# One level of Strassen's algorithm in the gate and up projections of a hybrid decoder block

## The chip, the cores and the metric

The kernel runs on one core of a Trainium2 chip. The metric is the device time of one execution in microseconds (us). The engines are TensorE (PE in the profile; its weight loads are PEld), VectorE (DVE), ScalarE (ACT), GpSimd (POOL) and SyncE (SP), whose queue issues all loads and stores here. A partition is one of the 128 lanes of the on-chip memory SBUF; matmuls write to accumulators in another memory, PSUM, in banks of 512 columns.

## The reference

One decoder block on 512 tokens of 1024 features. A mixer (retention and forgetting attention, merged by sigmoid gates) is followed by a SwiGLU feed-forward part with 2816 inner features, all in float32:

```python
    x = x + merged @ w_out[l]

    h2 = rmsnorm(x, g_ffn[l])
    ff = (jax.nn.silu(h2 @ w_gate[l]) * (h2 @ w_up[l])) @ w_down[l]
    x = x + ff
```

`rmsnorm(x, g)` divides each token's row by its root mean square and multiplies by the gains g. The change touches the two products with `w_gate` and `w_up`, each 512 x 1024 by 1024 x 2816, and what feeds and reads them.

## The kernel before, in words

To reach float32 accuracy, every float32 factor of a large product is split into a high part (a cast to the format fp32r, on ScalarE) and a low part (the value less its high part, on VectorE). One product of two tiles is then three matmuls into one accumulator (`three`, L156): high by high, high by low, low by high. Each matmul has its own weight load.

From the output projection on, features lie on partitions and tokens are the 512 moving columns; the weights are stationary, 128 x 128 at a time. `feat` (L507) makes two tiles of 128 output features: it loads the weights in units of four k-tiles (128 x 1024, 512 KB, `load_w` L133), splits each (`split_raw` L139: cast on L143, subtraction on L144), and goes over the eight k-tiles of 128 features of the input, 8 x 2 x 3 = 48 matmuls of 512 columns, two accumulators of one bank each. `three` calls `mm` (L70), so all matmuls stand on L71 in the profile.

The stages that matter here:

- Output projection (L642 to L664): four calls of `feat`. At the end of each, `evac_o` adds the residual on VectorE (L654), multiplies by the feed-forward gains and casts on ScalarE (L655, the tile `xgh`), makes the low part on VectorE (L656, `xgl`), squares on ScalarE (L661) and adds the squares into `sqs` on GpSimd (L662).
- Gate and up (L668 to L698): 11 pairs of feature tiles. For each pair `feat` makes the gate, then up, 22 calls in all. `evac_g` multiplies the gate's accumulator by `r2`, the inverse root mean square per token, on VectorE (L678) and applies silu on ScalarE (L679). `evac_u` multiplies up by `r2` on VectorE (L684), and GpSimd multiplies the two into `pf` (L685), two operations of 512 columns per pair. `r2` is made during the first gate from `sqs` by a matmul with ones and Newton's steps on tiles of 128 x 512 (L692, L693).
- Down projection (L700 to L725): for each of 22 k-tiles the weights and `pf` are split (L710 to L714), and 24 matmuls go to eight accumulators.

The order of instructions within an engine is made by the language's scheduler from the data's dependences and the order in the program; each engine then works through its own list in that order and stands still where the next one waits. The buffers of a tile name (a tag) are used in turn; a new tile waits until all readers of the one in its place are done.

Of the kernel before, what the change touches and what calls it, by code (L numbers as in the profile page):

```python
# [9 lines left out]
F32 = mybir.dt.float32  # L10
# [42 lines left out]
def block_kernel(ctx: ExitStack, tc, x, xT, c_early, c_tab, c_late, w_qf, w_tok, w_a, w_y, w_o, w_gu, w_dn, out):  # L53
# [27 lines left out]
    hp = tc.alloc_tile_pool(name="hp", bufs=1, side="left")  # L81
# [4 lines left out]
    sm = ctx.enter_context(tc.tile_pool(name="sm", bufs=2, side="right"))  # L86
    orp = tc.alloc_tile_pool(name="orp", bufs=1, side="right")
# [14 lines left out]
    def rsqrt(dst, ss, inv_n, shape, nm, pool=None):  # L102
        """(ss * inv_n + eps) ** -0.5 on the Vector engine: a guess from the exponent, then Newton's steps."""
        v = (pool or sm).tile(shape, F32, name=nm + "v", tag=nm + "v", bufs=1 if pool else 2)
        yi = (pool or sm).tile(shape, I32, name=nm + "y", tag=nm + "y", bufs=1 if pool else 2)
        a = (pool or sm).tile(shape, F32, name=nm + "a", tag=nm + "a", bufs=1 if pool else 2)
        y = yi.bitcast(F32)
        ts(out=v, in0=ss, scalar1=inv_n, scalar2=EPS, op0=ALU.mult, op1=ALU.add)
        ts(out=yi, in0=v.bitcast(I32), scalar1=1, scalar2=None, op0=ALU.logical_shift_right)
        ts(out=yi, in0=yi, scalar1=-1.0, scalar2=float(0x5F3759DF), op0=ALU.mult, op1=ALU.add)  # L110
        for i in range(3):
            stt(out=a, in0=y, scalar=-0.5, in1=y, op0=ALU.mult, op1=ALU.mult)
            tt(out=a, in0=a, in1=v, op=ALU.mult)
            stt(out=dst if i == 2 else y, in0=a, scalar=1.5, in1=y, op0=ALU.add, op1=ALU.mult)

# [107 lines left out]
    def tok_group(src, evac, cuts=(512,), ahead=()):  # L223
        """A projection with tokens on partitions: columns in cuts of one bank, src the units of 1024 / cut k-tiles each."""
# [20 lines left out]
    class Fill:  # L245
# [152 lines left out]
    def head_norm(z):  # L398
        """The heads' root mean squares: collected over the token tiles, applied after the last."""
# [36 lines left out]
    def fox_prep(a, part):  # L436
        """q or k of a pair of heads, with features on partitions, in high and low parts."""
# [21 lines left out]
    def fox_scores(a, e, i):  # L459
        """A block of queries of a head, the last block first: its row of the softmax, normalised."""  # L460
# [23 lines left out]
    def fox_turn(a, e, i):  # L484
        """That row with the keys on partitions: blocks j = 0..i at columns j*384 + i*128."""
# [21 lines left out]
    def feat(src, nu, mh, ml, evac):  # L507
        """Two tiles of features: src the units of 4 k-tiles each."""
# [130 lines left out]
    orp.release()  # L639

# [1 line left out]
    xp = tc.alloc_tile_pool(name="xp", bufs=1, side="right")  # L642
    xgh = xp.tile([P, NK, S], F32R, name="xgh")
    xgl = xp.tile([P, NK, S], F32R, name="xgl")
    x1 = xp.tile([P, NK, S], F32, name="x1")
    r2 = xp.tile([P, S], F32, name="r2")
    sqs = xp.tile([P, S], F32, name="sqs")
    for i in range(4):
        nc.sync.dma_start(out=x1[:, 2 * i:2 * i + 2, :], in_=xT[:, 2 * i:2 * i + 2, :])
    for mp in range(4):  # L650
        def evac_o(m2, acc):
            m = 2 * mp + m2
            xn = x1[:, m, :]
            tt(out=xn, in0=acc, in1=xn, op=ALU.add)  # L654
            act(out=xgh[:, m, :], in_=xn, func=AF.Copy, scale=gffn(m))  # L655
            stt(out=xgl[:, m, :], in0=xn, scalar=gffn(m), in1=f32(xgh)[:, m, :], op0=ALU.mult, op1=ALU.subtract)  # L656
            if m == 0:
                act(out=sqs, in_=xn, func=AF.Square)
            else:
                sq2 = xp.tile([P, S], F32, name="sq2", tag="sq2", bufs=2)  # L660
                act(out=sq2, in_=xn, func=AF.Square)  # L661
                gp.tensor_tensor(out=sqs, in0=sqs, in1=sq2, op=ALU.add)  # L662
        run(feat(lambda u: w_o[mp, u], 2, mgh, mgl, evac_o))
    mgp.release()  # L664
    hp.release()

# [1 line left out]
    fp = tc.alloc_tile_pool(name="fp", bufs=1, side="left")  # L668
    pf = fp.tile([P, NF, S], F32, name="pf")
    raw_pools += [fp]  # L670
    part_pools += [fp, fp]
    turns[:] = [0, 0]
    for f2 in range(NF // 2):
        gts = []

        def evac_g(m2, acc):
            gt = fp.tile([P, S], F32, name="gt", tag="fa", bufs=5)
            tt(out=gt, in0=acc, in1=r2, op=ALU.mult)  # L678
            act(out=gt, in_=gt, func=AF.Silu)  # L679
            gts.append(gt)  # L680

        def evac_u(m2, acc):
            up = fp.tile([P, S], F32, name="up", tag="fb", bufs=5)
            tt(out=up, in0=acc, in1=r2, op=ALU.mult)  # L684
            gp.tensor_tensor(out=pf[:, 2 * f2 + m2, :], in0=up, in1=gts[m2], op=ALU.mult)  # L685

        if f2 == 0:
            waiting = []
            for n, _ in enumerate(feat(lambda u: w_gu[0, f2, u], 2, xgh, xgl, lambda m2, acc: waiting.append(acc))):
                if n == 9:  # L690
                    pb = bank("tp")
                    mm(pb, lhsT=ones, rhs=sqs, start=True, stop=True)  # L692
            rsqrt(r2, pb, 1.0 / D, [P, S], "n2", xp)  # L693
            for m2, acc in enumerate(waiting):
                evac_g(m2, acc)
        else:
            run(feat(lambda u: w_gu[0, f2, u], 2, xgh, xgl, evac_g))
        run(feat(lambda u: w_gu[1, f2, u], 2, xgh, xgl, evac_u))  # L698
# [9 lines left out]

    for k in range(NF):
        h, l = split_w(w_dn[k])  # L710
        ph = fp.tile([P, S], F32R, name="ph", tag="fa", bufs=5)
        pl = fp.tile([P, S], F32R, name="pl", tag="fb", bufs=5)
        nc.scalar.copy(out=ph, in_=pf[:, k, :])
        tt(out=pl, in0=pf[:, k, :], in1=f32(ph), op=ALU.subtract)  # L714
        parts.append((h, l, ph, pl))
# [3 lines left out]
    for m in range(NK):  # L719
        for k in range(NF - TAIL, NF):  # L720
            down(k, m)
        ot = fp.tile([P, S], F32, name="ot", tag="fa", bufs=5)
# [3 lines left out]
    fp.release()  # L726
    xp.release()
    ps.release()
    drp.release()
    wp.release()  # L730
# [4 lines left out]
def _constants():  # L735
# [6 lines left out]
    ex = lambda a: np.exp(a.astype(f).astype(np.float64)).astype(f)  # noqa: E731  # L742
# [23 lines left out]
def _layout(i):  # L766
# [13 lines left out]
    def fm(m):  # L780
        """[K, N] -> [N/256, K/512, 128, 4*256]"""
        k, n = m.shape
        return m.reshape(k // 512, 4, P, n // 256, 256).transpose(3, 0, 2, 1, 4).reshape(n // 256, k // 512, P, 1024)

    qf = np.zeros((4, P, 4 * 264), f)
    for u in range(4):
# [12 lines left out]
        "w_gu": np.stack([fm(a["w_gate"][0]), fm(a["w_up"][0])]),  # L799
        "w_dn": a["w_down"][0].reshape(NF, P, D),  # L800
# [19 lines left out]
```

## Time and profile before

| What | Value |
| --- | --- |
| median time of 3 runs (753.85 to 753.88) | 753.86 us |
| span of the profiled execution | 750.1 us |
| time less span: what lies around it | 3.76 us |
| output projection and what is around it, 345.0 to 376.5 | 31.5 us |
| gate and up, 376.5 to 623.7 | 247.2 us |
| down projection and the end, 623.7 to 750.0 | 126.3 us |

The profile shows one execution, its span from the first to the last instruction; the execution's own time outside the profiler is not given, so the median stands for it. A row of a group gives the source line, the engine, the operation, output<-inputs with partitions x columns, the number of instructions, then the busy time in us, the mean ns of one, and the idle time of the engine ahead of them with what ended it. A row of a tile gives the least, median and longest duration in ns. A row of a timeline gives the start, the length of the merged instructions and, in brackets, the idle time before and what ended it.

### The profile page before, as it was taken

The page shows a single profiled execution, that of the slowest core. Times are in us where ns is not written, and L with a number is a line of the kernel's source. Part 1 is how long each engine was busy: PE and PEld are TensorE (multiplying, and loading weights), DVE is VectorE, ACT ScalarE, POOL GpSimd, SP SyncE. Part 2 cuts the span into 40 slices and gives each one's busy share as a digit, 9 for nine tenths or more (in the row PEclk, how much of TensorE's full clock was granted, in tenths as well). Part 3 has the DMA queues.
Part 4 walks back from the last instruction along what each step waited for, and adds up shares of the span by engine and source line. Part 5 has one row for each costly group of instructions (what it writes and reads, how often), then busy time and mean ns, then how long its engine had stood idle before and what let it go on. Part 6 is the DMA issues. An engine that isn't in the chain of part 4 may idle for free.

```text
span 750.1 us, 8828 instructions
## 1 busy us (share of the span) xinstructions
PE 742.7 (99%) x3430; PEld 596.9 (80%) x3430; DVE 367.7 (49%) x630; ACT 259.8 (35%) x389; POOL 110.0 (15%) x112
## 2 busy tenths in 40 slices
PE   8999999999999999999999999999999999999998
PEld 5888997878777788888878888888888887888886
DVE  6424567757878644454585333334334236323212
ACT  4532442447676622223333222222122233222210
POOL 0243502212222000000311110111111011000000
PEclk9999999999999999999999999999999999999999
DMA  8532221242320132235243232232232322222203
GB/s 306 207 128 76 78 85 56 85 124 75 113 85 29 57 107 90 86 97 210 91 154 121 86 109 87 90 107 85 95 102 84 100 98 84 96 101 84 85 0 113
DMA packets 23354, 76.20 MB, mean 102 GB/s; under 512 B 2697, under 2 KB 3081, under 8 KB 23313
## 3 DMA queue, kind: packets, MB, share of 16 engines
q1 hardware_dynamic: 23312, 75.64, 30.1%
q8 instruction: 27, 0.44, 0.2%
q14 instruction: 15, 0.11, 0.1%
HBM read 73.52 MB, written 2.11 MB: 101 GB/s over the span
## 4 chain that ended last, share of the span: by engine, by line
PE 93%; DVE 3%; ACT 2%; issue 1%; DMA 1%; SPq 0%; DVEq 0%; ACTq 0%
PE acc L71 76%; PE sc L71 9%; PE tp L71 6%; PE tp L74 2%; DVE wl L144 1%; ACT pr L479 1%; DMA xf<-in_xT_dram 1%; DVE pr L477 0%; ACT wh L143 0%; ACT pT L496 0%; DVE pr L481 0%; DVE tq L456 0%; ACT tq L455 0%; DVE up L684 0%; ACT tk L446 0%
## 5 line engine op out<-in xcount | busy, mean ns | idle before, releaser
L143 ACT CAST wh<-raw 128x1024 fp32r<-128x1024 f32 (+1 forms) x118 | 123.6, 1050 | 393.3 <-PE acc L71 323.3
L144 DVE TENSOR_TENSOR wl<-raw,wh 128x1024 fp32r<-128x1024 f32 (+1 forms) x118 | 153.3, 1300 | 201.3 <-ACT wh L143 199.9
L71 PE MATMUL acc<-xgh,wh 128*128 128x512 f32 x352 | 139.5, 396 | 0.0
L71 PE MATMUL acc<-xgh,wl 128*128 128x512 f32 x352 | 139.2, 395 | 0.0
L71 PE MATMUL acc<-xgl,wh 128*128 128x512 f32 x352 | 138.8, 394 | 0.0
L71 PEld LDWEIGHTS acc<-xgh,wl 128*128 128x128 f32 x352 | 66.2, 188 | 16.1
L71 PEld LDWEIGHTS acc<-xgl,wh 128*128 128x128 f32 x352 | 66.0, 188 | 16.3 <-issue 0.2
L71 PEld LDWEIGHTS acc<-xgh,wh 128*128 128x128 f32 x352 | 66.1, 188 | 15.8 <-issue 0.2
L71 PE MATMUL acc<-wh,xh 128*128 128x512 f32 (+2 forms) x192 | 70.3, 366 | 0.0
L685 POOL TENSOR_TENSOR pf<-up,gt 128x512 f32<-128x512 f32 x22 | 38.3, 1760 | 206.0 <-DVE up L684 206.0
L71 PE MATMUL acc<-wl,xh 128*128 128x512 f32 (+2 forms) x192 | 68.4, 356 | 0.0
L71 PE MATMUL acc<-wh,xl 128*128 128x512 f32 (+2 forms) x192 | 68.3, 356 | 0.0
L71 PE MATMUL acc<-xh,wh 128*128 128x512 f32 x128 | 52.0, 406 | 0.0
L71 PE MATMUL acc<-xh,wl 128*128 128x512 f32 x128 | 50.7, 396 | 0.0
L71 PE MATMUL acc<-xl,wh 128*128 128x512 f32 x128 | 50.5, 395 | 0.0
L71 PEld LDWEIGHTS acc<-wh,xh 128*128 128x128 f32 x192 | 36.1, 188 | 5.9 <-issue 0.3
L71 PEld LDWEIGHTS acc<-wh,xl 128*128 128x128 f32 x192 | 36.1, 188 | 5.7
L71 PEld LDWEIGHTS acc<-wl,xh 128*128 128x128 f32 x192 | 36.1, 188 | 4.7
L71 PE MATMUL acc<-pl,wh 128*128 128x512 f32 x88 | 34.5, 392 | 0.0
L71 PE MATMUL acc<-ph,wl 128*128 128x512 f32 x88 | 34.5, 392 | 0.0
L71 PE MATMUL acc<-ph,wh 128*128 128x512 f32 x88 | 34.3, 393 | 0.0
L662 POOL TENSOR_TENSOR sqs<-sqs,sq 128x512 f32<-128x512 f32 x7 | 11.6, 1651 | 127.4 <-ACT sq L661 127.2
(215 smaller groups left out, 1127.2 us busy)
## 6 DMA issues: line engine op xcount, KB each, us to landing
raw<-in_w_gu_dram SPq DMA_DIRECT2D x44, 512.0 KB, 3.5
raw<-in_w_dn_dram SPq DMA_DIRECT2D x22, 512.0 KB, 3.5
raw<-in_w_tok_dram SPq DMA_DIRECT2D x16, 512.0 KB, 3.7
raw<-in_w_a_dram SPq DMA_DIRECT2D x16, 512.0 KB, 3.5
raw<-in_w_y_dram SPq DMA_DIRECT2D x8, 512.0 KB, 3.5
raw<-in_w_o_dram SPq DMA_DIRECT2D x8, 512.0 KB, 3.6
xf<-in_xT_dram SPq DMA_DIRECT2D x8, 256.0 KB, 5.8
xs<-in_x_dram SPq DMA_DIRECT2D x2, 1024.0 KB, 9.3
```

The source lines that it names most:

```text
L71: in_order(nc.tensor.matmul(o, **kw))
L74: in_order(nc.tensor.transpose(out=o, in_=src, identity=ident))
L143: nc.scalar.copy(out=h[:, :width], in_=raw[:, :width])
L144: tt(out=l[:, :width], in0=raw[:, :width], in1=f32(h)[:, :width], op=ALU.subtract)
L479: fox["last"] = act(out=pr[:, :n], in_=pr[:, :n], func=AF.Exp, scale=-1.0, bias=nm, accum_out=rs)
L662: gp.tensor_tensor(out=sqs, in0=sqs, in1=sq2, op=ALU.add)
L685: gp.tensor_tensor(out=pf[:, 2 * f2 + m2, :], in0=up, in1=gts[m2], op=ALU.mult)
```

## The change

Gate and up are made by one level of Strassen's algorithm, in the form of Winograd (seven products, with sums that share parts). The weights of one call are seen as 2 x 2 blocks (the two k-tiles of a pair by the two feature tiles), the activations likewise (the two k-tiles of a pair by two halves of 256 tokens). Eight block products become seven, each 4 k-pairs x 3 matmuls = 12 matmuls of 256 columns: 84 where there were 48 of 512.

- Activations: `evac_o` leaves x1 with its gains in `fx`; per pair of k-tiles VectorE makes the four combinations S1 to S4 (256 columns each), and the seven blocks are split in two goes of three and four slots (`split_x`: cast on ScalarE, subtraction on VectorE). This is done once, beside and behind the output projection.
- Weights: `factors` loads 1 MB (four blocks of 512 columns) for one step, that is gate or up of one pair of feature tiles. VectorE makes four combinations T1 to T4, and the three plain blocks and the four combinations are split: casts of 1536, 1024 and 1024 columns on ScalarE, subtractions of the same size on VectorE. The tiles `raw`, `ah` and `al` (plain blocks) have two buffers, `ts`, `ch0`, `cl0` (T2, T1) and `ch1`, `cl1` (T4, T3) one each. `factors` for step n + 1 stands in the program ahead of the products of step n.
- Products: `winograd` runs three single products, then T2 x S2 into the accumulator x that ScalarE has copied out once (`u`), T1 x S1 into z, T3 x S3 into x after a second copy, T4 x A22 into y, and a third copy. VectorE makes the outputs `d` from y, z and the copies in three operations (512, 256, 512 columns).
- The multiplications by `r2` leave VectorE: for the gate GpSimd multiplies `d` by `r2`, ScalarE applies silu, GpSimd multiplies by `r2` again; for up GpSimd multiplies by `d`. These are three operations of 1024 columns per pair. `r2` comes from four matmuls of one column and Newton's steps on 128 x 4.
- The first step takes the products over the first three k-pairs ahead of those over the fourth.
- Around it: `xh` and `xl` and the new pools lie elsewhere in memory; the down projection's weights come two k-tiles to a load, its parts use the buffers of `ch0`, `ah`, `ch1`, `ah` in turn.

The core of the diff:

```diff
     for mp in range(4):
+        fx = tmp.tile([P, 8, HT], F32, name="fx", tag="fx")
...
         run(feat(lambda u: w_o[mp, u], 2, mgh, mgl, evac_o))
+        split_x(mp, fx, 0, 3)
+        tt(out=fx[:, S1, :], in0=fx[:, A21, :], in1=fx[:, A22, :], op=ALU.subtract)
+        tt(out=fx[:, S2, :], in0=fx[:, S1, :], in1=fx[:, A11, :], op=ALU.subtract)
+        tt(out=fx[:, S3, :], in0=fx[:, A11, :], in1=fx[:, A21, :], op=ALU.subtract)
+        tt(out=fx[:, S4, :], in0=fx[:, S2, :], in1=fx[:, A12, :], op=ALU.add)
+        split_x(mp, fx, 3, 7)
...
+    def factors(src):
+
+        raw, ts4 = wtile("raw"), wtile("ts")
+        nc.sync.dma_start(out=raw, in_=src)
+        a = split_to(raw[:, 1:4, :], ("ah", "al"))
+        tt(out=ts4[:, 1:4:2, :], in0=raw[:, 1:4:2, :], in1=raw[:, 0:1, :].broadcast_to([P, 2, 512]), op=ALU.add)
+        tt(out=ts4[:, T2, :], in0=ts4[:, T1, :], in1=raw[:, B22, :], op=ALU.add)
+        c0 = split_to(ts4[:, 0:2, :], ("ch0", "cl0"))
+        tt(out=ts4[:, T4, :], in0=ts4[:, T2, :], in1=raw[:, B21, :], op=ALU.add)
+        c1 = split_to(ts4[:, 2:4, :], ("ch1", "cl1"))
+        return {"B11": (a, 0), "B21": (a, 1), "B22": (a, 2), "T2": (c0, 0), "T1": (c0, 1), "T4": (c1, 0), "T3": (c1, 1)}
+
+    def product(o, w, slot, new, js=range(4)):
+        (h, l), i = w
+        for j in js:
+            fs = slice(j * P, (j + 1) * P)
+            for n, (st, mv) in enumerate(((h, xfh), (h, xfl), (l, xfh))):
+                first = new and j == 0 and n == 0
+                mm(o, lhsT=st[:, i, fs], rhs=mv[j][:, slot, :], start=first, stop=j == 3 and n == 2, skip_group_check=not new)
+
+    def winograd(w, early=False):
+
+        x, y, z = bank("sc"), bank("acc"), bank("acc")
+        u = fp.tile([P, 3, HT], F32, name="u", tag="u", bufs=2)
+        d = fp.tile([P, 2, S], F32, name="d", tag="d", bufs=3)
+        lo, hi = slice(0, HT), slice(HT, S)
+        singles = ((x[:, lo], w["B11"], A11), (y[:, lo], w["B21"], A12), (z[:, hi], w["B22"], S4))
+        for js in ((range(3), range(3, 4)) if early else (range(4),)):
+            for o, f, s in singles:
+                product(o, f, s, True, js)
+        nc.scalar.copy(out=u[:, 0, :], in_=x[:, lo])
+        product(x[:, lo], w["T2"], S2, False)
+        product(z[:, lo], w["T1"], S1, True)
+        nc.scalar.copy(out=u[:, 1, :], in_=x[:, lo])
+        product(x[:, lo], w["T3"], S3, False)
+        product(y[:, hi], w["T4"], A22, True)
+        nc.scalar.copy(out=u[:, 2, :], in_=x[:, lo])
+        tt(out=d[:, 1, :].rearrange("p (s t) -> p s t", s=2), in0=z[:, lo].rearrange("p (o t) -> p o t", o=1).broadcast_to([P, 2, HT]), in1=u[:, 1:3, :], op=ALU.subtract)
+        tt(out=d[:, 1, lo], in0=z[:, hi], in1=d[:, 1, lo], op=ALU.add)
+        tt(out=d[:, 0, :].rearrange("p (s t) -> p s t", s=2), in0=y.rearrange("p (s t) -> p s t", s=2), in1=u[:, 0:3:2, :], op=ALU.add)
+        return d
...
+    for n in range(NF):
+        f2, g = n // 2, n % 2
+        if n < NF - 1:
+            ws.append(factors(w_gu[(n + 1) % 2, (n + 1) // 2]))
+        d = winograd(ws[n], n == 0)
...
+        pp = pf[:, 2 * f2:2 * f2 + 2, :]
+        if g == 0:
+            gp.tensor_tensor(out=d, in0=d, in1=r2b, op=ALU.mult)
+            act(out=pp, in_=d, func=AF.Silu)
+            gp.tensor_tensor(out=pp, in0=pp, in1=r2b, op=ALU.mult)
         else:
-            run(feat(lambda u: w_gu[0, f2, u], 2, xgh, xgl, evac_g))
-        run(feat(lambda u: w_gu[1, f2, u], 2, xgh, xgl, evac_u))
+            gp.tensor_tensor(out=pp, in0=pp, in1=d, op=ALU.mult)
```

More of the change, by code (lines that the diff above doesn't have):

```diff
@@ L80, in block_kernel @@
     wp = tc.alloc_tile_pool(name="wp", bufs=1, side="left")
-    hp = tc.alloc_tile_pool(name="hp", bufs=1, side="left")
     ftok = tc.alloc_tile_pool(name="ftok", bufs=1, side="left")
@@ L86, in block_kernel @@
     sm = ctx.enter_context(tc.tile_pool(name="sm", bufs=2, side="right"))
+    hp = tc.alloc_tile_pool(name="hp", bufs=1, side="right")
     orp = tc.alloc_tile_pool(name="orp", bufs=1, side="right")
@@ L639, in block_kernel, with split_x @@
     orp.release()
+    hp.release()
+    HT = S // 2
     xp = tc.alloc_tile_pool(name="xp", bufs=1, side="right")
-    xgh = xp.tile([P, NK, S], F32R, name="xgh")
-    xgl = xp.tile([P, NK, S], F32R, name="xgl")
     x1 = xp.tile([P, NK, S], F32, name="x1")
     r2 = xp.tile([P, S], F32, name="r2")
-    sqs = xp.tile([P, S], F32, name="sqs")
+    xfh = [xp.tile([P, 7, HT], F32R, name="xfh", tag=f"xfh{j}") for j in range(4)]
+    xfl = [xp.tile([P, 7, HT], F32R, name="xfl", tag=f"xfl{j}") for j in range(4)]
+    wq = tc.alloc_tile_pool(name="wq", bufs=1, side="right")
+    tmp = tc.alloc_tile_pool(name="tmp", bufs=1, side="left")
+    sqs = r1
+    A11, A12, A22, S1, S2, S3, S4, A21 = range(8)
     for i in range(4):
         nc.sync.dma_start(out=x1[:, 2 * i:2 * i + 2, :], in_=xT[:, 2 * i:2 * i + 2, :])
+    def split_x(j, f, lo, hi):
+        nc.scalar.copy(out=xfh[j][:, lo:hi, :], in_=f[:, lo:hi, :])
+        tt(out=xfl[j][:, lo:hi, :], in0=f[:, lo:hi, :], in1=f32(xfh[j])[:, lo:hi, :], op=ALU.subtract)
     for mp in range(4):
+        fx = tmp.tile([P, 8, HT], F32, name="fx", tag="fx")
         def evac_o(m2, acc):
@@ L654, in evac_o @@
             tt(out=xn, in0=acc, in1=xn, op=ALU.add)
-            act(out=xgh[:, m, :], in_=xn, func=AF.Copy, scale=gffn(m))
-            stt(out=xgl[:, m, :], in0=xn, scalar=gffn(m), in1=f32(xgh)[:, m, :], op0=ALU.mult, op1=ALU.subtract)
+            act(out=fx[:, 0:8:7, :] if m2 == 0 else fx[:, 1:3, :], in_=xn.rearrange("p (s t) -> p s t", s=2), func=AF.Copy, scale=gffn(m))
             if m == 0:
@@ L659, in evac_o @@
             else:
-                sq2 = xp.tile([P, S], F32, name="sq2", tag="sq2", bufs=2)
+                sq2 = tmp.tile([P, S], F32, name="sq2", tag="sq2")
                 act(out=sq2, in_=xn, func=AF.Square)
@@ L663, in block_kernel @@
         run(feat(lambda u: w_o[mp, u], 2, mgh, mgl, evac_o))
+        split_x(mp, fx, 0, 3)
[4 more added lines that the diff above has]
+        split_x(mp, fx, 3, 7)
+    B12, B11, B21, B22 = range(4)
+    T2, T1, T4, T3 = range(4)
@@ new lines, in block_kernel, with wtile, split_to @@
+    wpools = [wq]
+    WT = {"raw": (4, F32), "ts": (4, F32), "ah": (3, F32R), "al": (3, F32R),
+          "ch0": (2, F32R), "cl0": (2, F32R), "ch1": (2, F32R), "cl1": (2, F32R)}
+    seen = {}
+    def wtile(tag):
+        n, dt = WT[tag]
+        two = tag in ("raw", "ah", "al") and len(wpools) > 1
+        i = seen.get(tag, 0)
+        seen[tag] = i + 1
+        return wpools[i % 2 if two else 0].tile([P, n, 512], dt, name=tag, tag=tag)
+    def split_to(src, tags):
+        h, l = wtile(tags[0]), wtile(tags[1])
+        nc.scalar.copy(out=h, in_=src)
+        tt(out=l, in0=src, in1=f32(h), op=ALU.subtract)
+        return h, l
@@ L664, in block_kernel @@
+    ws = [factors(w_gu[0, 0])]
+    tmp.release()
     mgp.release()
-    hp.release()
+    wp.release()
     fp = tc.alloc_tile_pool(name="fp", bufs=1, side="left")
+    wpools += [fp]
     pf = fp.tile([P, NF, S], F32, name="pf")
[L670 to L695, printed above, removed]
-        else:
-            run(feat(lambda u: w_gu[0, f2, u], 2, xgh, xgl, evac_g))
-        run(feat(lambda u: w_gu[1, f2, u], 2, xgh, xgl, evac_u))
@@ new lines, in block_kernel @@
+    r2b = r2.rearrange("p (o t) -> p o t", o=1).broadcast_to([P, 2, S])
+    for n in range(NF):
[3 more added lines that the diff above has]
+        d = winograd(ws[n], n == 0)
+        if n == 0:
+            pb = bank("tp")
+            for t in range(NT):
+                mm(pb[:, t:t + 1], lhsT=sqs[:, t * P:(t + 1) * P], rhs=ones[:, 0:1], start=True, stop=True)
+            rstd2 = sm.tile([P, NT], F32, name="rstd2", tag="rstd2", bufs=1)
+            rsqrt(rstd2, pb[:, 0:NT], 1.0 / D, [P, NT], "n1")
+            broadcast_cols(rstd2, r2)
+        pp = pf[:, 2 * f2:2 * f2 + 2, :]
[3 more added lines that the diff above has]
+            gp.tensor_tensor(out=pp, in0=pp, in1=r2b, op=ALU.mult)
+        else:
+            gp.tensor_tensor(out=pp, in0=pp, in1=d, op=ALU.mult)
@@ L707, in down @@
         three(accs[m], h[:, fs], l[:, fs], ph, pl, k == 0, k == NF - 1)
+    raw = None
     for k in range(NF):
[L710 to L715, printed above, removed]
+        if k % 2 == 0:
+            raw = wtile("raw")
+            nc.sync.dma_start(out=raw, in_=w_dn[k // 2])
+        src = raw[:, 2 * (k % 2):2 * (k % 2) + 2, :]
+        tags = (("ch0", "cl0"), ("ah", "al"), ("ch1", "cl1"), ("ah", "al"))[k % 4]
+        h, l = (wtile(t)[:, 0:2, :] for t in tags)
+        nc.scalar.copy(out=h, in_=src)
+        tt(out=l, in0=src, in1=f32(h), op=ALU.subtract)
+        hl = fp.tile([P, 2, S], F32R, name="hl", tag="d", bufs=3)
+        nc.scalar.copy(out=hl[:, 0, :], in_=pf[:, k, :])
+        tt(out=hl[:, 1, :], in0=pf[:, k, :], in1=f32(hl)[:, 0, :], op=ALU.subtract)
+        h, l = (a.rearrange("p a b -> p (a b)") for a in (h, l))
+        parts.append((h, l, hl[:, 0, :], hl[:, 1, :]))
         if k < NF - TAIL:
@@ L721, in block_kernel @@
             down(k, m)
-        ot = fp.tile([P, S], F32, name="ot", tag="fa", bufs=5)
+        ot = fp.tile([P, S], F32, name="ot", tag="u", bufs=2)
         for cs in (slice(0, S),) if m < NK - 1 else (slice(0, S // 2), slice(S // 2, S)):
@@ L726, in block_kernel @@
     fp.release()
+    wq.release()
     xp.release()
@@ L729, in block_kernel @@
     drp.release()
-    wp.release()
     cst.release()
@@ L783, in fm, with wino @@
         return m.reshape(k // 512, 4, P, n // 256, 256).transpose(3, 0, 2, 1, 4).reshape(n // 256, k // 512, P, 1024)
+    def wino(m):
+        k, n = m.shape
+        v = m.reshape(k // 256, 2, P, n // 256, 2, P)
+        v = np.stack([v[:, 0, :, :, 1], v[:, 0, :, :, 0], v[:, 1, :, :, 0], v[:, 1, :, :, 1]])
+        return v.transpose(3, 2, 0, 1, 4).reshape(n // 256, P, 4, k // 2)
     qf = np.zeros((4, P, 4 * 264), f)
@@ L798, in _layout @@
         "w_o": fm(a["w_out"][0]),
-        "w_gu": np.stack([fm(a["w_gate"][0]), fm(a["w_up"][0])]),
-        "w_dn": a["w_down"][0].reshape(NF, P, D),
+        "w_gu": np.stack([wino(a["w_gate"][0]), wino(a["w_up"][0])]),
+        "w_dn": a["w_down"][0].reshape(NF // 2, 2, P, 2, D // 2).transpose(0, 2, 1, 3, 4).reshape(NF // 2, P, 4, D // 2),
     }
```

## The prediction

> **What bounds the kernel now.** I read the page first, for the share of each engine and the chain that ended last.
>
> ```profile
> span 750.1 us, 8828 instructions
> PE 742.7 (99%) x3430; PEld 596.9 (80%) x3430; DVE 367.7 (49%) x630; ACT 259.8 (35%) x389; POOL 110.0 (15%) x112
> PE 93%; DVE 3%; ACT 2%; issue 1%; DMA 1%; SPq 0%; DVEq 0%; ACTq 0%
> ```
>
> TensorE is busy for all but 7.4 us of the span, and it is 93% of the chain. But these are averages, so next comes the view of busy time by stretch. The three stretches are the output projection, gate and up, and the down projection:
>
> ```profile
> core 0: us, PE busy (x) PEld busy (x) DVE busy (x) ACT busy (x) POOL busy (x), PEclk, DMA share, GB/s
> 345.00:376.50 31.50, 31.50 (x138) 25.64 (x137) 15.85 (x17) 11.46 (x16) 8.13 (x5) 1.00 0.35 117
> 376.50:623.70 247.20, 247.20 (x1060) 198.90 (x1059) 101.51 (x105) 64.85 (x76) 38.71 (x22) 1.00 0.31 100
> 623.70:750.00 126.30, 122.31 (x529) 98.83 (x527) 43.52 (x51) 28.98 (x37) 2.98 (x2) 0.99 0.23 79
> ```
>
> Gate and up take 247.2 us, and TensorE never pauses there, at a granted clock of 1.00. They are 22 steps (11 pairs of feature tiles, gate and up each) of 48 matmuls with 512 moving columns: 1056 matmuls, 234 ns each, 11.24 us a step. VectorE works 101.5 of the 247 us and GpSimd 38.7. That room is what the change spends.
>
> **TensorE's part.** A step becomes 84 matmuls of 256 columns: seven products of four k-pairs, three partial products each. The q projection already runs such matmuls, a new weight load before each. The timeline of TensorE has 38 of them in a row; these are the first and the last:
>
> ```profile
> 82.52 0.28 PE L71 MATMUL acc<-wl,xh 128*128 128x256 f32 x1
> 86.88 0.28 PE L71 MATMUL acc<-wh,xl 128*128 128x256 f32 x1
> ```
>
> 37 intervals in 4.36 us are 117.8 ns, half of 234. Weight loads do not get in the way at this size. So 22 x 84 x 117.8 ns = 217.7 us: TensorE alone would save 29.5 us.
>
> **VectorE's part.** Every step now makes four more weight combinations and splits seven blocks in place of four. Per step and partition VectorE does, with both inputs in SBUF: the low part of three blocks (1536 columns), T1 and T3 (1024), T2 (512), the low part of T2 and T1 (1024), T4 (512), the low part of T4 and T3 (1024). Then, from PSUM, three sums: 512, 256 and 512 columns. The rows that price these:
>
> ```profile
> L144 DVE TENSOR_TENSOR wl<-raw,wh 128x1024 fp32r<-128x1024 f32 x3 | 3.7, 1225 | 4.0 <-ACT wh L143 4.0
> L714 DVE TENSOR_TENSOR pl<-pf,ph x22: 680/684/1760, 624.5 to 720.8; 128x512 fp32r<-128x512 f32 x22
> L684 DVE TENSOR_TENSOR up<-acc,r 128x512 f32<-128x512 f32 x22 | 15.2, 692 | 28.5 <-PE acc L71 28.5
> L340 DVE TENSOR_TENSOR sT<-sc,cl 128x256 f32<-128x256 f32 x8 | 3.0, 420 | 5.1 <-PE sc L71 5.0
> 345.54 1.41 DVE L656 SCALAR_TENSOR_TENSOR xgl<-x,ce,xgh 128x512 fp32r<-128x512 f32 x2
> ```
>
> From 1225 ns for 1024 columns and a median of 684 for 512 (in the view of the tile pf), 512 more cost 541, so 1536 columns are 1.77 us. The six SBUF operations are 1.77 + 3 x 1.225 + 2 x 0.684 = 6.81 us, the three sums 0.692 + 0.420 + 0.692 = 1.80: together 8.61. Back to back, two operations overlap by 0.08 us (two of 745 in 1.41); were all six to do so it would be 8.13. Some depend on the one ahead, so I take 8.4 us, 6.6 of it weights. That is under TensorE's 9.90 (84 x 117.8 ns): alone, VectorE would be hidden.
>
> **GpSimd's part decides.** Before, GpSimd multiplied two tiles of 512 columns per gate-and-up pair. Now it does three of 1024: the gate's sum by r2, its silu by r2, and the product with up. How VectorE and GpSimd get on stands in the views of the tiles xgl and pf and in the timelines:
>
> ```profile
> L656 DVE SCALAR_TENSOR_TENSOR xgl<-x,ce,xgh x8: 743/745/1789, 345.5 to 379.8; 128x512 fp32r<-128x512 f32 x8
> 356.71 2.45 DVE L656 SCALAR_TENSOR_TENSOR xgl<-x,ce,xgh 128x512 fp32r<-128x512 f32 x2
> 356.81 3.49 POOL L662 TENSOR_TENSOR sqs<-sqs,sq 128x512 f32<-128x512 f32 x2 [8.72 <-ACT sq L661]
> L685 POOL TENSOR_TENSOR pf<-up,gt x22: 1290/1520/2283, 400.3 to 625.3; 128x512 f32<-128x512 f32 x22
> 488.97 1.39 DVE L684 TENSOR_TENSOR up<-acc,r 128x512 f32<-128x512 f32 x2 [2.78 <-PE acc L71]
> 489.80 3.52 POOL L685 TENSOR_TENSOR pf<-up,gt 128x512 f32<-128x512 f32 x2 [18.86 <-DVE up L684]
> 490.56 1.62 DVE L144 TENSOR_TENSOR wl<-raw,wh 128x1024 fp32r<-128x1024 f32 x1 [0.20 <-ACT wh L143]
> L309 POOL TENSOR_TENSOR ta<-rz,cl 128x256 f32<-128x256 f32 x4 | 3.0, 738 | 28.1 <-ACT rz L273 28.0
> ```
>
> At 345 us, with GpSimd idle, two xgl took 1.41; at 356.7, beside one GpSimd operation that got in between, 2.45, so VectorE lost 1.04 us to it. At 490 the same happens to the low part of a weight (1.62 for 1.225), and GpSimd's second multiplication takes up to 2.28 where 1.29 is its least. But the two operations at 488.97 that read an accumulator in PSUM took 1.39, undisturbed. So an operation with both inputs in SBUF and one of GpSimd take turns, and only the sums from PSUM can lie beside GpSimd.
>
> By size, GpSimd takes 738 ns for 256 columns and 1290 for 512, so 2.39 us for 1024, and VectorE's loss grows from 1.04 to 2.14. Three of these per pair of steps are 6.4 us. Can they lie beside the sums? The first follows its own sum, so the next operation on VectorE is a weight's. The second follows silu: at the latest 0.14 for the hand-off, 1.77 waiting for a VectorE operation, 2.39, and silu, about 1.05, some 5.4 us after the sum. The next sums are six weight operations (6.6) and a turn (2.14) away. The third follows up's sum like the first. So I count no overlap:
>
> two steps: 2 x 8.4 + 6.4 = 23.2 us, 11.6 a step, against TensorE's 9.90 and the 11.24 of before.
>
> The Trainium skill, page "SBUF — State Buffer", section "SBUF: two separate sides", says that VectorE with two SBUF inputs and GpSimd contend for one pair of ports, an exclusive lock held for the whole instruction, the loser fully blocked. Charged with the whole 2.39 of each GpSimd operation, the sum by the page would be 8 us longer than mine over 32 of them, about 774; the 1.04 of the row is shorter than the 1.29 of the operation, and I go by the row.
>
> **ScalarE.** Its rows:
>
> ```profile
> L143 ACT CAST wh<-raw 128x1024 fp32r<-128x1024 f32 x3 | 3.1, 1049 | 9.0 <-PE acc L71 9.0
> L713 ACT CAST ph<-pf 128x512 fp32r<-128x512 f32 x22 | 13.3, 615 | 1.7 <-POOL pf L685 1.7
> L496 ACT COPY pT<-tp 128x256 f32<-128x256 f32 x8 | 2.9, 365 | 1.4 <-PE tp L74 1.2
> ```
>
> Casts of 1536, 1024 and 1024 columns are 1.48 + 2 x 1.05 us, three copies out of PSUM 3 x 0.365, silu 0.52 a step on average: 5.2 of 11.6 us. The second copy must end while TensorE does the product T1 x S1 (12 x 117.8 ns = 1.41 us), or TensorE waits; 0.37 fits unless a cast or a waiting silu stands ahead of it.
>
> **DMA.** The bytes are the same, in 22 transfers of 1 MB instead of 44 of half; at 100 GB/s in this stretch, nothing. One place is late: the second step's raw weights go into memory that the output projection's operands hold, so SyncE's queue stands there until 376.3, with the third step's load behind it.
>
> ```profile
> raw<-in_w_gu_dram SPq DMA_DIRECT2D x44, 512.0 KB, 3.5
> ```
>
> At twice 3.5 us they land by 383.3, when VectorE still has x to split (below), so this is hidden; uncovered it would cost up to 7 us once.
>
> **The start of the stage.** Before, x's last tile was split beside running matmuls. Now the last tile pair has to be summed into S1 to S4 before any product over the fourth k-pair:
>
> ```profile
> 376.23 1.39 DVE L654 TENSOR_TENSOR x<-acc,x 128x512 f32<-128x512 f32 x2 [2.78 <-PE acc L71]
> L655 ACT ACTIVATE xgh<-x,ce 128x512 fp32r<-128x512 f32 x8 | 5.7, 713 | 0.0
> L661 ACT ACTIVATE sq<-x 128x512 f32<-128x512 f32 x7 | 4.3, 615 | 0.0
> ```
>
> From 376.2: residual 1.4, the second gain copy 0.9 later (713 ns and the hand-off), a square 0.6, the cast of three slots (768 columns) 0.83, their low part 0.95, four sums of 256 columns 4 x 0.41, a cast 1.05, a low part 1.23: 8.6 us, with one square's turn on GpSimd (1.04) hidden in what can be reordered; 7 at best, 10 at worst. TensorE has 33 matmuls (3.9 us) meanwhile, so it waits some 4.5 us. Weights of the first step are prepared earlier, beside the output projection, where VectorE is half idle (15.85 of 31.5 us).
>
> **The sum.** VectorE from 376.3 on: 8.7 until x is split, then 21 weight sets x 6.6 = 138.6, 21 sums x 1.8 = 37.8, 32 turns x 2.14 = 68.5, and twelve small operations for r2, priced by this row at 12 x 0.295 = 3.5:
>
> ```profile
> L112 DVE SCALAR_TENSOR_TENSOR n4a<-n4y 128x4 f32<-128x4 f32 x12 | 3.5, 295 | 0.4
> ```
>
> Together 248.4. Then TensorE's last two products, 2.8. The end of the stage is at 376.3 + 8.7 + 248.4 + 2.8 = 636.2, against 623.7: +12.5 us. The down projection has the same matmuls; its 4.0 us of waiting (126.30 less 122.31) I leave. Stages ahead only move in memory: nothing. Span 762.6. The median of 753.86 lies 3.8 above the span of 750.1, so 766.4: **766 us**. Own range of this case: 759 (all operations overlapping, 21 x 0.27, and x split in 7) to 778 (none overlapping, 21 x 0.21, and the turns as long as the whole operation, 32 x 0.25).
>
> **The rivals.**
> *TensorE keeps the pace* (chance 0.18): if GpSimd's operations find VectorE idle or at its sums, two steps need no more than 19.8. Then 753.9 - 29.5 + 4.5 = 729. It decides from the point where 3.4 of the 6.4 us per pair are hidden. Against it: the order of dependence above, and that the sums offer only 3.6.
> *Half hidden* (0.15): silu comes late, and its second multiplication falls on the next sums: 1.8 saved per pair, 11 x 1.8 = 20 us: 745, with the scatter of the terms 740 to 755.
> *ScalarE's queue* (0.09): silu at the head of ScalarE waits for GpSimd, the second copy stands behind it, and TensorE for that; 1 to 2 us in each of 11 gates on top of my sum: 777 to 788.
> *Matmuls of 256 columns at the pace of their weight loads* (0.02): each load lasts 188 ns, 1848 x 188 = 347 us, +100: 854. The 117.8 ns speak against it.
>
> ```profile
> L71 PEld LDWEIGHTS acc<-xgh,wh 128*128 128x128 f32 x352 | 66.1, 188 | 15.8 <-issue 0.2
> ```
>
> **How the numbers follow.** The forecast has 0.56. A measurement tells 0.2% (1.5 us) from no change. Slower: the forecast without its lowest part (0.51), ScalarE's queue and the loads: 0.62. Within 0.2%: 0.03 each from forecast and half hidden: 0.06. Faster: 0.18, 0.12 and 0.02 from the forecast: 0.32. The range 733 to 780 leaves out over half of the first rival (0.10) and the upper ends (0.07 to 0.08).
>
> **What would show it.** Right: VectorE over 90% busy between 385 and 636, its SBUF operations with maxima 2 us over their minima, GpSimd's of 1024 columns near 2.4 at least; TensorE pausing in each step, ended by VectorE's low part of T4 and T3 (or T2 and T1); about 11.6 us a step; a pause of 4 to 5 us near 380. Wrong: TensorE at 99% with steps of 9.9, or pauses ended by ScalarE's copies.

## The result, and the profile after

The changed kernel takes 761.26 us (median of 4 runs, 760.69 to 761.47) against 753.86 before: slower, the ratio of the runs on record 1.0108 with a 95% interval of 1.0093 to 1.0123 (the two medians alone give 1.0098). The forecast was 766 us, slower.

The first lines of the page of the changed kernel, span and busy time of each engine:

```profile
span 759.0 us, 10565 instructions
PE 727.8 (96%) x4232; PEld 629.5 (83%) x4232; DVE 527.2 (69%) x760; ACT 320.1 (42%) x475; POOL 170.5 (22%) x123
```

TensorE has lost 14.9 us of work and the span has grown by 8.9: it waits now. VectorE has gained 159.5 us and GpSimd 60.5. Averages over the span do not say who sets the pace, so next comes the busy time by stretch (the output projection, two pieces of the stage's start, its body, the down projection):

```profile
core 0: us, PE busy (x) PEld busy (x) DVE busy (x) ACT busy (x) POOL busy (x), PEclk, DMA share, GB/s
345.00:376.50 31.50, 31.50 (x137) 25.66 (x136) 28.71 (x32) 18.44 (x24) 7.71 (x5) 1.00 0.34 123
376.50:384.00 7.50, 5.94 (x47) 5.61 (x46) 6.48 (x9) 4.26 (x6) 2.55 (x2) 1.00 0.00 0
384.00:386.00 2.00, 2.00 (x12) 2.00 (x11) 1.74 (x9) 0.84 (x2) 0.00 (x0) 0.52 0.46 70
390.00:628.00 238.00, 217.19 (x1734) 214.06 (x1733) 230.63 (x191) 105.65 (x137) 95.38 (x31) 0.97 0.27 94
634.10:759.00 124.90, 120.02 (x529) 98.71 (x527) 46.19 (x54) 30.55 (x40) 2.71 (x1) 1.00 0.27 93
```

In the body VectorE is busy for 230.6 of 238 us, 97%: it is full. Gate and up now end at 634.1, 257 us after the output projection's end where it was 247 before. From step 1 to step 21 the timeline of TensorE gives the pace; these are the first matmuls of the two steps:

```profile
392.68 0.38 PE L71 MATMUL sc<-xfh,ah 128*128 128x256 f32 x1 [1.01 <-ACT ah L701]
623.68 0.28 PE L71 MATMUL sc<-xfh,ah 128*128 128x256 f32 x1
```

20 steps in 231.0 us are 11.55 each; 11.6 was forecast.

What fills VectorE is seen in its groups between 390 and 620 us, with GpSimd's three multiplications (the columns are those of the groups before):

```profile
L710 DVE TENSOR_TENSOR ts<-raw 128x1024 f32<-128x1024 f32 x21 | 59.0, 2810 | 1.1 <-DMA raw<-in_w_gu_dram 0.6
L702 DVE TENSOR_TENSOR cl<-ts,ch 128x1024 fp32r<-128x1024 f32 x40 | 49.8, 1250 | 0.8 <-ACT ch L701 0.8
L702 DVE TENSOR_TENSOR al<-raw,ah 128x1536 fp32r<-128x1536 f32 x20 | 38.1, 1907 | 1.9 <-ACT ah L701 1.9
L713 DVE TENSOR_TENSOR ts<-ts,raw 128x512 f32<-128x512 f32 x20 | 32.4, 1619 | 0.6
L711 DVE TENSOR_TENSOR ts<-ts,raw 128x512 f32<-128x512 f32 x21 | 18.7, 889 | 0.7
L769 POOL TENSOR_TENSOR d<-d,r 128x1024 f32<-128x1024 f32 x10 | 32.3, 3234 | 80.9 <-DVE d L744 62.0 <-ACT r L220 18.9
L771 POOL TENSOR_TENSOR pf<-pf,r 128x1024 f32<-128x1024 f32 x10 | 27.8, 2783 | 12.6 <-ACT pf L770 12.6
L773 POOL TENSOR_TENSOR pf<-pf,d 128x1024 f32<-128x1024 f32 x10 | 32.5, 3254 | 50.7 <-DVE d L744 41.2 <-DVE d L743 9.5
```

Two groups of the same shape, `ts` and `cl` with 1024 columns, take 2810 and 1250 ns: the first stands where GpSimd's turn falls, the second hardly ever. The busy time of VectorE holds waiting. The three sums from PSUM keep their length throughout. None of them ran beside a multiplication in this kernel, so that they could do so undisturbed is shown by the kernel before alone (the two of 488.97 in the prediction). This is the view of the tile d, least, median and longest:

```profile
L742 DVE TENSOR_TENSOR d<-acc,u x22: 674/678/691, 391.3 to 634.4; 128x512 f32<-128x512 f32 x22
L744 DVE TENSOR_TENSOR d<-acc,u x22: 673/681/685, 395.9 to 635.9; 128x512 f32<-128x512 f32 x22
```

The view of the waits, though, names another cause of TensorE's pauses (engine and line waiting <- what ended it: us in total, times, longest):

```profile
PE sc L71 <- ACT u L738: 17.2, 8, 4.3
PE sc L71 <- DVE cl L702: 2.1, 3, 1.0
```

The second copy of the accumulator x on ScalarE ends most pauses, and VectorE few. The timelines of one step show why (step 11, from 508 us on):

```profile
511.66 3.31 POOL L769 TENSOR_TENSOR d<-d,r 128x1024 f32<-128x1024 f32 x1 [7.08 <-DVE d L744]
512.75 3.31 DVE L710 TENSOR_TENSOR ts<-raw 128x1024 f32<-128x1024 f32 x1
515.00 1.06 ACT L770 ACTIVATE pf<-d 128x1024 f32<-128x1024 f32 x1 [5.04 <-POOL d L769]
515.97 1.45 ACT L701 CAST ah<-raw 128x1536 fp32r<-128x1536 f32 x1
516.14 2.86 POOL L771 TENSOR_TENSOR pf<-pf,r 128x1024 f32<-128x1024 f32 x1 [1.17 <-ACT pf L770]
516.82 2.73 DVE L713 TENSOR_TENSOR ts<-ts,raw 128x512 f32<-128x512 f32 x1
517.33 0.36 ACT L738 COPY u<-sc 128x256 f32<-128x256 f32 x1
517.74 0.58 PE L71 MATMUL sc<-xfh,ch 128*128 128x256 f32 x1 [2.44 <-ACT u L738]
```

GpSimd's first multiplication holds VectorE's `ts` until 515; silu on ScalarE waits for it, a cast of 1.45 us follows, then the copy, and TensorE has stood 2.44 us. So two theories were to be told apart. The turns theory, the forecast's: VectorE and GpSimd take turns, and their sum is the pace, whoever ends TensorE's pauses. The chain theory, the rival of ScalarE's queue: TensorE waits because silu waits for GpSimd with the copy behind it. It costs 17 to 19 us whatever VectorE's load.

### The profile page after: what moved, and what is told of

Read it like the earlier page. It is cut to its first block, busy times and chain, and to the rows that moved or that the text cites. A ratio compares the mean times of both kernels' runs of the same rounds, so it can differ in the third digit from the quotient of the medians.

```text
span 759.0 us, 10565 instructions
## 1 busy us (share of the span) xinstructions
PE 727.8 (96%) x4232; PEld 629.5 (83%) x4232; DVE 527.2 (69%) x760; ACT 320.1 (42%) x475; POOL 170.5 (22%) x123
## 4 chain that ended last, share of the span: by engine, by line
PE 71%; DVE 14%; issue 5%; POOL 4%; ACT 4%; DMA 1%; SPq 0%; DVEq 0%; ACTq 0%; POOLq 0%
PE acc L71 48%; PE sc L71 15%; PE tp L71 6%; POOL d L769 4%; DVE cl L702 3%; PE tp L74 2%; DVE ts L710 2%; DVE al L702 2%; ACT ah L701 1%; DVE d L742 1%; DVE d L744 1%; DVE d L743 1%; DVE ts L711 1%; DMA out_dram<-ot 1%; DMA raw<-in_w_tok_dram 1%
## 5 line engine op out<-in xcount | busy, mean ns | idle before, releaser
L143 ACT CAST wh<-raw 128x1024 fp32r<-128x1024 f32 (+1 forms) x52 | 54.5, 1050 | 128.2 <-PE acc L71 100.7
L144 DVE TENSOR_TENSOR wl<-raw,wh 128x1024 fp32r<-128x1024 f32 (+1 forms) x52 | 67.8, 1305 | 46.1 <-ACT wh L143 45.9
L71 PE MATMUL sc<-xfh,ch 128*128 128x256 f32 x176 | 53.2, 302 | 17.7 <-ACT u L738 17.2
L710 DVE TENSOR_TENSOR ts<-raw 128x1024 f32<-128x1024 f32 x22 | 60.2, 2737 | 1.1 <-DMA raw<-in_w_gu_dram 0.6
L702 DVE TENSOR_TENSOR cl<-ts,ch 128x1024 fp32r<-128x1024 f32 x44 | 54.6, 1247 | 0.8 <-ACT ch L701 0.8
L71 PE MATMUL sc<-xfh,cl 128*128 128x256 f32 x176 | 52.0, 295 | 2.1 <-DVE cl L702 2.1
L71 PE MATMUL sc<-xfl,ch 128*128 128x256 f32 x176 | 51.8, 294 | 0.0
L71 PE MATMUL acc<-xfh,ch 128*128 128x256 f32 x176 | 51.2, 291 | 0.0
L71 PE MATMUL acc<-xfl,ch 128*128 128x256 f32 x176 | 50.8, 289 | 0.0
L71 PE MATMUL acc<-xfh,cl 128*128 128x256 f32 x176 | 50.7, 288 | 0.0
```

The source lines that it names most:

```text
L71: in_order(nc.tensor.matmul(o, **kw))
L143: nc.scalar.copy(out=h[:, :width], in_=raw[:, :width])
L144: tt(out=l[:, :width], in0=raw[:, :width], in1=f32(h)[:, :width], op=ALU.subtract)
L702: tt(out=l, in0=src, in1=f32(h), op=ALU.subtract)
L710: tt(out=ts4[:, 1:4:2, :], in0=raw[:, 1:4:2, :], in1=raw[:, 0:1, :].broadcast_to([P, 2, 512]), op=ALU.add)
```

## The experiments

All changes are to the changed kernel. Times are medians; ratios are to the kernel before, on the same chip (752.5 to 753.2 us there).

**Silu freed from GpSimd.** The multiplication keeps its size and place but writes aside.

```diff
-            gp.tensor_tensor(out=d, in0=d, in1=r2b, op=ALU.mult)
+            aside = pf[:, 2 * f2 + 2:2 * f2 + 4, :] if f2 < NF // 2 - 1 else d
+            gp.tensor_tensor(out=aside, in0=d, in1=r2b, op=ALU.mult)
             act(out=pp, in_=d, func=AF.Silu)
```

> Silu reads the sums directly; GpSimd's first multiplication by r2 still runs, at the same size, into a part of pf that is written again later, so silu lacks r2. Turns theory (VectorE and GpSimd take turns, and their sum of 23.1 us per two steps is the pace): nothing is taken off either engine, so 755 to 762 us; VectorE's idle 7 us in the stage is the most there is to win. Chain theory (TensorE waits because silu waits for GpSimd and the second copy stands behind silu on ScalarE): the 17 to 19 us that TensorE waited for that copy go, about 742 us.

761.44 us (761.17 to 762.63), the changed kernel's time. The chain is broken and nothing is won: TensorE now pauses ahead of T2 x S2 instead, for 15.0 us in 9 waits ended by the first copy. A pause's releaser is the last in a row of things that are all late. VectorE stays full, 207.05 of 210 us:

```profile
390.00:600.00 210.00, 192.05 (x1543) 188.61 (x1542) 207.05 (x169) 92.77 (x123) 87.19 (x27) 0.98 0.27 92
```

**Memsets for multiplications.** Here `d` stands for the gate's and up's sum.

```diff
-            gp.tensor_tensor(out=d, in0=d, in1=r2b, op=ALU.mult)
+            for _ in range(3):
+                gp.memset(d, 1.0)
             act(out=pp, in_=d, func=AF.Silu)
-            gp.tensor_tensor(out=pp, in0=pp, in1=r2b, op=ALU.mult)
+            for _ in range(3):
+                gp.memset(pp, 1.0)
         else:
-            gp.tensor_tensor(out=pp, in0=pp, in1=d, op=ALU.mult)
+            for _ in range(3):
+                gp.memset(d, 1.0)
```

> Each of GpSimd's three multiplications is replaced by three memsets of the same 1024 columns, which read nothing from SBUF; silu still waits for the first of them, and the feed-forward part comes out wrong. A memset of 64 x 512 took 0.52 us, so three of 1024 columns are an estimated 2.5 to 3 us, as long as a multiplication. Turns theory: with nothing read, VectorE does not stop, its 8.4 us a step fit, and TensorE sets the pace at 10.08 a step: about 731 us. Chain theory: silu waits as long as before, 753 to 761 us. If memsets too make VectorE stop, as before: 761.

732.06 us, ratio 0.9722 (0.9705 to 0.9738): 29 us off. Silu still waits for GpSimd, three memsets of 955 ns or 2.9 us, and TensorE does not pause for it. But its waits are half as long as in the changed kernel (21.8 us in 11 against 42.4 in 10), so this run by itself does not clear silu. The stretch and the groups of this kernel:

```profile
390.00:600.00 210.00, 208.77 (x1736) 208.19 (x1736) 175.22 (x191) 107.80 (x138) 88.82 (x93) 1.00 0.31 106
L710 DVE TENSOR_TENSOR ts<-raw 128x1024 f32<-128x1024 f32 x21 | 25.7, 1224 | 0.8 <-DMA raw<-in_w_gu_dram 0.3
L713 DVE TENSOR_TENSOR ts<-ts,raw 128x512 f32<-128x512 f32 x21 | 14.5, 692 | 0.6
L770 POOL MEMSET d<- 128x1024 f32 x33 | 31.5, 955 | 83.2 <-DVE d L744 67.0 <-ACT u L735 14.9
```

GpSimd is busy for 88.8 us, VectorE's `ts` takes 1224 ns where it took 2810, and TensorE is busy for 208.8 of 210. So GpSimd's busy time alone does not stop VectorE. What the memsets leave out is the reading of SBUF; they are shorter operations too, and no run parts the two. This is also the time at which the first rival of the prediction (TensorE keeps the pace, 729 us) would have come true.

**Less of VectorE alone.** The low parts of the plain blocks are left out.

```diff
-        a = split_to(raw[:, 1:4, :], ("ah", "al"))
+        ah = wtile("ah")
+        nc.scalar.copy(out=ah, in_=raw[:, 1:4, :])
+        a = ah, ah
```

> The low parts of the three plain weight blocks are left out (the third matmul of each of their products takes the high part again), 1.76 us of VectorE a step; GpSimd, silu, the copies and all matmuls stay. Turns theory: 3.5 us less per two steps, so TensorE's 20.2 per two becomes the pace: 730 to 736 us. Chain theory: GpSimd's first multiplication, silu and the copy stand as they stood: 756 to 761 us.

739.44 us, ratio 0.9817 (0.9803 to 0.9832): 21.8 us off, where the chain theory had at most 5. That bound took silu's waits as unchanged, though, and they fell to 29.6 us in 10. The time stops 3.4 us short of what the turns theory gave: step 3 has a pause of 3.1 us and, with a slow clock after it, takes 14.8, and from then on every other step takes 10.45 and not 10.08.

**One turn less: r2 applied at the end.** This computes the same function.

```diff
             act(out=pp, in_=d, func=AF.Silu)
-            gp.tensor_tensor(out=pp, in0=pp, in1=r2b, op=ALU.mult)
...
-            tt(out=ot[:, cs], in0=accs[m][:, cs], in1=x1[:, m, cs], op=ALU.add)
+            tt(out=ot[:, cs], in0=accs[m][:, cs], in1=r2[:, cs], op=ALU.mult)
+            tt(out=ot[:, cs], in0=ot[:, cs], in1=x1[:, m, cs], op=ALU.add)
```

> The second multiplication by r2 is taken off GpSimd (11 of 33 operations): r2 is one factor per token, so it is applied to the eight tiles of the down projection's result on VectorE instead. The same function is computed. Turns theory: 11 turns of 2.14 us less, 0.7 us more at the end: 738 to 742 us, faster than the kernel before the change. Chain theory: the first multiplication, silu and the copy are untouched: 756 to 761 us.

746.09 us (743.8 to 747.8), ratio 0.9903 (0.9881 to 0.9924): faster than the kernel before. 15 us off, not 19 to 23. VectorE is still full (134.21 of 136 us between 464 and 600), two steps take 20.83 us, about its sum (21.1), but a single pause of 4.5 us near 445, with a slow clock after it, takes the rest: silu waits for GpSimd, the copy behind it. Here, where VectorE is nearly down to TensorE's pace, the chain does cost.

**Silu behind the copy.** As the run before, with an order on ScalarE.

```diff
+            held = d
         else:
+            after(act(out=pp, in_=held, func=AF.Silu), marks[-1])
             gp.tensor_tensor(out=pp, in0=pp, in1=d, op=ALU.mult)
```

`marks` holds the second copies of `winograd`.

> As the run with r2 applied at the end, and silu is ordered on ScalarE behind the next step's second copy, so that no copy stands behind a silu that waits for GpSimd. The same function is computed. Turns theory: two steps need 2 x 8.4 + 2 x 2.14 = 21.1 us of VectorE (20.8 measured without the order), TensorE 20.2; the order can win only the one long pause near 450 us with its slow clock after it, some 6 us: 739 to 743. Chain theory: all pauses before the third product go (7.0 us in 8 waits, and the slow clock after the long one), two steps take 20.2: 735 to 738.

741.8 us, ratio 0.9849 (0.9834 to 0.9863): 4.3 us less, in the turns theory's range. Between 390 and 600 us VectorE is idle for 4.1 us, where it was idle for 8.0 without the order (6.5 when that kernel was run again). Later it is as full as there:

```profile
464.00:600.00 136.00, 134.24 (x1102) 132.49 (x1101) 134.22 (x118) 62.85 (x85) 42.77 (x14) 1.00 0.30 101
```

**The second step's weights placed first.** `factors` of step 1 is called ahead of the allocation of `pf`.

> As the run with the order, and the second step's raw weights are given a place that is free before the output projection's end: their load was issued at 384.65 us, when the last split of x had given its memory back, and landed at about 389.3. Both theories: step 0, 15.7 us from first product to the next step's, loses the wait for the second step's weights, 1.3 us and more, so 1.5 to 3 us less than the run with the order. If the load's place were no cause: no change.

741.98 us, no change, but this tells nothing: the load was still issued at 386.4, when the last split of x had ended. The edit did not move it. What that load costs stays open.

**One turn more.**

```diff
             gp.tensor_tensor(out=pp, in0=pp, in1=r2b, op=ALU.mult)
+            gp.tensor_tensor(out=pp, in0=pp, in1=r2b, op=ALU.mult)
```

> The kernel after the change with a fourth multiplication of 1024 columns per pair on GpSimd (the gate by r2 once more, so the feed-forward part has a factor r2 too many). Turns theory: 11 turns of 2.14 us more: 783 to 786 us. Chain theory: the added one lies behind silu, on nobody's path but GpSimd's, which is half idle: 761 to 764 us.

785.94 us, ratio 1.0435 (1.0420 to 1.0451): 24.7 us for 11 more operations on an engine that was 22% busy over the span, 2.24 each; VectorE is busy 245.32 of 250 us. This run and the first are the two that part the theories: there the chain was broken and nothing was won, here only GpSimd got more to do, TensorE's waits for the second copy grew by 7.2 us (24.4 for 17.2), and the time by 24.7. With 0, 22, 33 and 44 such operations the times are 732, 746, 761 and 786: where VectorE is full, every one counts; below that TensorE's pace is the floor.

**The squares off GpSimd.** As the run with the order, and the last two tiles of squares go to TensorE.

```diff
+            elif m >= 6:
+                last.append(tmp.tile([P, S], F32, name="sq3", tag=f"sq{m}"))
+                act(out=last[-1], in_=xn, func=AF.Square)
...
-                mm(pb[:, t:t + 1], lhsT=sqs[:, t * P:(t + 1) * P], rhs=ones[:, 0:1], start=True, stop=True)
+                for i, sq in enumerate(last):
+                    mm(pb[:, t:t + 1], lhsT=sq[:, t * P:(t + 1) * P], rhs=ones[:, 0:1], start=i == 0, stop=i == 2)
```

> As the run with the order (741.8 us), and the last two of the seven additions of squares leave GpSimd: TensorE adds these two tiles in the small matmuls for r2. The same function is computed. In the kernel after the change these two additions stopped VectorE for 0.6 and 1.1 us in the chain that splits the last tiles of x, and held ScalarE for 0.8; TensorE paused 2.8 us there and then ran 3 us at half the granted clock. If the turns are what lengthens the start: the chain ends 1.5 to 2 us earlier, the pause is about 1.3 us, and without a long pause the clock stays up: 2 to 4 us less, 738 to 740. If the chain's own operations are the length: within 1 us of 741.8.

740.6 us (740.49 to 741.69), ratio 0.9842 (0.9829 to 0.9856), between the two expectations. It is 1.2 us under the run with the order, but that one's ratio on its own chip, 0.9849, lies within this interval: no gain is shown. The turns are gone (all four sums of x take 0.43 us), TensorE's one pause of 2.8 us has become two of 1.0 and 1.5, and the clock is 1.00 behind them:

```profile
384.00:386.00 2.00, 2.00 (x19) 2.00 (x19) 0.89 (x2) 0.00 (x0) 0.00 (x0) 1.00 0.00 0
```

The changed kernel has 12 matmuls at a granted clock of 0.52 there. Step 0 is 1.3 us shorter (14.4 for 15.7), but the squares are not shown to be the cause. The next run, without them, has the pause of 2.8 us unchanged, and with the clock at 1.00 behind it its step 0 takes 14.4 us as well. Here VectorE's list had the first small operation for r2 ahead of the last split, and stood there for 1.9 us.

**The run with r2 at the end, once more.**

> The kernel with r2 applied at the end once more, on the same chip as the run with the squares, to stand beside it: 744 to 748 us.

747.89 us, ratio 0.9935 (0.9922 to 0.9949); the two readings, 746.1 and 747.9, are 1.8 apart, so the order's gain is 4 to 6 us. The two profiles of this one kernel differ at the start. Both have the pause of 2.8 us; the first time (first line) the clock halved behind it and step 0 took 15.7 us, the second time (second line) it did not, and step 0 took 14.4:

```profile
386.00:388.00 2.00, 2.00 (x12) 2.00 (x11) 1.66 (x11) 1.60 (x2) 0.00 (x0) 0.50 0.50 94
386.00:388.00 2.00, 2.00 (x18) 1.94 (x18) 1.85 (x6) 0.65 (x2) 0.00 (x0) 1.00 0.00 0
```

**That small operation behind the split.**

```diff
-            rsqrt(rstd2, pb[:, 0:NT], 1.0 / D, [P, NT], "n1")
+            rsqrt(rstd2, pb[:, 0:NT], 1.0 / D, [P, NT], "n1", behind=split)
```

> As the run with the squares on TensorE (740.6 us), and VectorE's first small operation for r2 is ordered behind the last split of x. There VectorE had stood 1.9 us at that operation, which waited for TensorE, with the last split behind it, ready and needed. The same function is computed. If that wait is what is left of the start: 1.5 to 2 us less, 738.5 to 739.5. If the start's length lies in the chain of sums and casts itself: within 0.5 us of 740.6.

741.08 us, no change. The split of x ends at 384.6 and not 386.4, yet step 0 takes 14.15 us: TensorE waits 1.0 us for the second step's cast, which stands on ScalarE behind the third copy, as it does in the changed kernel. The start has several limits near one another; which of them are worth having is not settled.

## Why the prediction was right

The mechanism and the sign were right, and the time was 4.7 us too long.

- *TensorE's part.* A step was to be 9.90 us at 117.8 ns; it is 10.08 at 120 (84 matmuls), the memset run's pace. Its own saving was real: 22 x (11.24 - 10.08) is 25.5 us, and the run without turns is 21 us faster than before (732.06 to 753.17).
- *VectorE's part.* 8.4 us a step; in the memset run 175.22 of 210 us at 10.08 a step are 8.41. The durations alone were 1.22, 0.69 and 0.42 for 1024, 512 and 256 columns, as taken.
- *The turns.* 2.14 us each was forecast. In step 11 above, `ts` takes 3.31 us for 1.22 and that of 516.82 takes 2.73 for 0.69: 2.1 and 2.0 us lost. The excess of VectorE's groups over the memset run's is 21 x 1.59 + 20 x 0.93 + 21 x 0.20 + 20 x 0.15 + 40 x 0.03 = 60 us for 30 operations: 2.0 each. The fourth one cost 2.24. That none would lie beside the sums held. The whole operation, 2.39, that the Trainium skill, page "SBUF — State Buffer", section "SBUF: two separate sides", would charge was too much by both, so the row was the better price. The section "Who interferes with whom" of the same page says that VectorE with two SBUF inputs contends with a GpSimd instruction that reads SBUF, not with one that only writes it; the memset run agrees (1224 ns for 2810).
- *The pace.* 11.55 us for 11.6 is closer than its terms. Per two steps VectorE was busy for 22.4 of 23.1 us, where 23.2 of work were forecast; the 0.7 us idle, which the sum had at nothing, make up the difference, by luck. Nor did TensorE pause in each step, as forecast: nearly every other one took 10.08 us, its own length.
- *ScalarE.* "0.37 fits unless a cast or a waiting silu stands ahead of it": they did stand ahead. I had named VectorE's low parts as what would end TensorE's pauses, and pauses ended by ScalarE's copies as a sign against me. That marker was wrong: with silu freed the pauses went to another copy and the time stayed. The rival's chain is there, but it showed a cost of its own only when turns had been taken off: the 4 to 6 us that the order won.
- *The start.* 4.5 us of waiting in one pause was forecast, and step 0 is 5.6 longer than a step. The pause near 380 is only 2.6 us (2.76 from matmul to matmul, less the 0.12 of one). A second wait, 1.0 near 392, was not in the sum: it is for the cast of the second step's weights, which stands on ScalarE behind the third copy. A third part, the slow clock, is 1.3 us (15.7 for 14.4) and comes in some executions only. That the waiting forecast is near the sum of these parts is luck. The load of the second step's weights I had issued at 376.3 and landed by 383.3; it was issued at 384.65, behind the last split of x, whose memory it takes. No cost of this is shown: VectorE read the weights at 389.39, and the cast began at 391.15, behind the third copy (390.88).
- *The sum.* The stage was to end at 636.2 and ends at 634.1 (turns of 2.0 for 2.14 are 4.5 us less, the start 1.1 more; 1.3 us between them are not accounted for). The down projection takes 124.9 for 126.4. What lies around the span is 2.3 for 3.8: the 3.76 of before set the median against the span of another execution, and where a time and its own span are both on record 1.7 to 2.2 us lie between them. Together 5.1 of 766.4, to 761.3.

## What to carry to other kernels

Before work goes to an engine because it looks half idle, add up what it shares: here two engines at 97% and 40% of a stretch were one queue, and the sum of their demands, 23.2 us per two steps, forecast the pace to 0.1 us, some of it by offsetting errors. A view of the waits names who came last, not who is full; the test is to take the named wait away, and then to take load away. When an algorithm trades matmuls for sums, look for factors that can leave the loop (r2 is one per token and passes through the down projection): that and an order on ScalarE made a loss of 1.1% a gain of 1.5%.

## What the runs showed of the hardware

After TensorE's pause near 381 (2.76 us from one matmul over a block of x to the next, a small matmul for r2 between) the granted clock was 0.52 between 384 and 386, and for some 3 us matmuls came 0.21 us apart where they are 0.12. The pause does not decide this alone: in the second profile of the kernel with r2 at the end, and in the run with silu freed, the same pause left the clock at 1.00. Of four pauses of 2.7 us in the changed kernel, those at 515, 561 and 606 were followed by the slow clock and the one at 492 was not. In the run with the squares, pauses of 1.0 and 1.5 us left it at 1.00, but one of 2.1 us from matmul to matmul, at 421, did not:

```profile
424.00:427.00 3.00, 3.00 (x16) 3.00 (x16) 3.00 (x3) 1.80 (x3) 0.00 (x0) 0.50 0.43 98
```

The Trainium skill, "TensorE: Matmul & The Clock Gate", section "HAM oscillation — how this bites in real kernels", gives gaps over about 3.4 us as the thing to avoid. Here shorter ones were enough in some executions; what decides between them is not shown.

A memset of 128 x 1024 on GpSimd takes 955 ns and does not slow VectorE; a product of the same size took between 2.4 and 3.3 us, and stopped VectorE's operations with two SBUF inputs. In the kernel before, operations with an input from PSUM kept their length beside one.
